# Neighbourhood attention: the softmax reciprocals of twelve of sixteen steps turned and spread by two transfers on Pool's queue in place of a PE transpose

## The chip, the cores and the metric

The kernel runs on one core of a Trainium2 chip. The metric is the device time of one launch in microseconds, the median of several runs; lower is better. The profile is one execution of the same program recorded by the hardware profiler, with its own time. The engines are named as in the profile: PE (matmul), PEld (PE's weight loads), DVE (vector), ACT (scalar), POOL (GpSimd) and SP (whose queue issues most loads).

## The reference, cut to what matters

The reference is a two-layer transformer on 256 latent tokens (a grid of 4 rows by 64 columns) and 256 context tokens, width 1024. Layer 0 mixes with retention, layer 1 with neighbourhood attention; each is followed by a squared-ReLU MLP and layer norms. The change lies in the neighbourhood attention of layer 1, with 32 heads of 32 columns:

```python
s_loc = einsum('bqhd,bikhd->bhqik', q_r, k_band) + bias      # -inf outside the window
s_ctx = einsum('bqhd,blhd->bhql', q_r, k_c)
s = concatenate([s_loc.reshape(...), s_ctx], axis=-1)
prob = softmax(s, axis=-1)
o = einsum('bhqik,bikhd->bqhd', p_loc, v_band) + einsum('bhql,blhd->bqhd', prob[..., band:], v_c)
y_lat = o.reshape(b, n, d) @ w_o
```

The softmax divides by a sum for each query and head. The kernel multiplies the attended values by the reciprocals of these sums at the end.

## The kernel before, in words

The attention is cut into 16 steps (`NS = 16`, line 1438). Step n stands for a group of four heads (g = n // 2) and half of the query columns (qt = n % 2), that is 128 queries on the partitions. What is done for one n:

- `scores(n)` (line 1547): twelve PE matmuls into four PSUM banks, one for each head (tile `pqk` in the profile).
- `soften(n)` (line 1560): DVE adds the bias and takes the minimum for each head, ACT takes the exponential and adds up each row. The result is `Es[n, j]` (tile `s`) and `sums[n]`, 128 queries by 4 heads.
- `invert(n)` (line 1586): DVE takes the reciprocal of `sums[n]` in place and a second DVE instruction copies each of the four columns 32 times into the tile `rr`, 128 by 128.
- `gather(n)` (line 1600): four Pool copies collect 8 columns of each row of the other half of the columns into one block (`pt`, place RAW), and `load_bias(n + 2)` issues four (n even) or eight (n odd) bias transfers on Pool's queue, into `bias` and `G`.
- `flip(n)` (line 1612): PE transposes the exponentials, twelve blocks and then the block that Pool gathered (tile `ppt`); ACT and DVE copy the four banks to `pt`. `flip_sums(n)` (line 1627) adds a fourteenth transpose: it turns `rr` and writes the result into the right part of one half of the PSUM bank `pav`. There each of the 128 rows (head, column of the head) holds the reciprocals of the 128 queries.
- `turned(n)` (line 1633): ACT copies this turned block from PSUM to the SBUF tile `rt`.
- `attend(n)` (line 1638): PE multiplies with the values into the left part of the same half of `pav` (13 matmuls, which the trace shows as 2 and then 24 instructions), DVE multiplies the result by `rt`, and `split` (ACT, then DVE) writes it into `oTh` and `oTl`, as a high and a low part.

The steps are pipelined over each other by the loop at line 1830. Pass n of it holds, in this order: `gather(n+1)`, `turned(n)`, weight loads, `scores(n+2)`, `soften(n+2)`, further PE work from the table `STEPS` (a projection of keys, queries or values, or half of the output projection), `flip(n+1)`, `invert(n+2)`, `attend(n)`. The thirteen passes n = 0 to 12 are written so; step 0 is prepared ahead of the loop, and n = 13 to 15 are closed by the code after it, from line 1848, where `flip_sums`, `turned` and `attend` are called one by one.

What sets the order: in this part of the kernel PE, ACT and DVE keep the order of the program (line 1400 to 1402 switch it on), and so does SP's queue (`PIN`, line 101). Pool does not: the framework orders its instructions, and the trace shows bias transfers between the gather copies. The transfers' waits and all semaphores are set by the framework from the tiles that each instruction reads and writes. The helper class at line 84 issues the instructions, so nearly all carry the line L84, and the tiles tell them apart.

Of the kernel before, what the change touches and what calls it, by code (L numbers as in the profile page):

```python
# [10 lines left out]
F32 = mybir.dt.float32  # L11
# [6 lines left out]
P = 128  # L18
# [9 lines left out]
HD = 32  # L28
# [76 lines left out]
def kernel(  # L105
# [23 lines left out]
    pe, act, dve, pool, sp = (  # L129
        InOrder(tc, getattr(nc, e), e in PIN)  # L130
        for e in ("tensor", "scalar", "vector", "gpsimd", "sync")
    )
# [3 lines left out]
    smp = ec(tc.tile_pool(name="smp", bufs=4))  # L136
# [6 lines left out]
    dram = ec(tc.tile_pool(name="dram", bufs=1, space=DRAM))  # L143
# [8 lines left out]
    def nm(s):  # L152
        uid[0] += 1
        return f"{s}_{uid[0]}"

    def bank(s="ps"):
        return psp.tile([P, 512], F32, tag="ps", name=nm(s))
# [8 lines left out]
    def tsl(t):  # L166
        return slice(t * P, (t + 1) * P)
# [90 lines left out]
    def fetch(n, in_scratch=False, at=None):  # L258

        for src, k, ncol in specs[len(units) : len(units) + max(n, 0)]:  # L260
            raw = rawp.tile([P, k, ncol], F32, tag="raw", name=nm("raw"))
            sp.dma_start(out=raw[:], in_=src.rearrange("(k p) n -> p k n", p=P))
            if len(units) in scaled_units:
                dve.tensor_mul(
                    out=raw[:], in0=raw[:], in1=scale_row[0].unsqueeze(1).broadcast_to([P, k, ncol])
                )
            if in_scratch or len(units) in scratch_units:
                hi, lo = Rows([scr("hi", F32R) for _ in range(k)]), Rows([scr("lo", F32R) for _ in range(k)])
                for i in range(k):
                    act.copy(out=hi[:, i, :], in_=raw[:, i, :])  # L270
                    pending.append((lo[:, i, :], raw[:, i, :], hi[:, i, :]))
                units.append((hi, lo))
                continue
            if at is None:
                hi = hip.tile([P, k, ncol], F32R, tag="hi", name=nm("hi"))
                lo = lop.tile([P, k, ncol], F32R, tag="lo", name=nm("lo"))
            else:
                both = slot(at, [P, 2, k, ncol], F32R, "hilo")
                hi, lo = both[:, 0], both[:, 1]
            act.copy(out=hi[:], in_=raw[:])  # L280
            pending.append((lo[:], raw[:], hi[:]))
            units.append((hi, lo))

    def lows(n=100, eng=None):
        for lo, raw, hi in pending[:n]:
            (eng or dve).tensor_sub(out=lo, in0=raw, in1=hi.bitcast(F32))
        del pending[:n]
# [591 lines left out]
    def part_v(k, a, b):  # L879
# [8 lines left out]
        out=lgn[:, 0], in_=ret_decay[0].rearrange("(o d) h -> o (d h)", o=1).broadcast_to([P, 8])  # L888
# [118 lines left out]
    for h in range(RH):  # L1007
# [102 lines left out]
        for t in range(4):  # L1110
            po = bank("po")
            scs = list(range(4)) if t < 2 else [2, 3]
            for i, sc in enumerate(scs):
# [9 lines left out]
                out=on, in0=po[:], scalar1=mv[:, 0:1], scalar2=r[:], op0=ALU.subtract, op1=ALU.mult  # L1123
# [314 lines left out]
    NS = 16  # L1438
# [106 lines left out]
    sums, rrs, Es, pts, pss = {}, {}, {}, {}, {}  # L1545

    def scores(n):

        g, qt = n // 2, n % 2
        pss[n] = [bank("pqk") for _ in range(4)]  # L1550
        q, k = q_of(g), kTs[g // 2][:, g % 2]
        for i, (a, b) in enumerate(((0, 0), (0, 1), (1, 0))):
            for j in range(4):
                js = slice(32 * j, 32 * j + 32)
                pe.matmul(
                    pss[n][j][:], lhsT=q[js, a, tsl(qt)], rhs=k[js, b, :], start=(i == 0), stop=(i == 2),
                    tile_position=(32 * j, 0),
                )

    def soften(n):  # L1560

        mn = smp.tile([P, 4], F32, tag="mn", name=nm("mn"), bufs=3)
        sm = sums[n] = smp.tile([P, 4], F32, tag="sums", name=nm("sums"), bufs=3)
        for j in range(4):
            s = Es[n, j] = scr("s")
            dve.tensor_tensor_reduce(
                out=s[:].rearrange("p (a t) -> p a t", a=2),
                in0=pss[n][j][:].rearrange("p (a t) -> p a t", a=2),
                in1=bias_ap(n, j),
                scale=1.0,  # L1570
                scalar=3.0e38,
                op0=ALU.add,
                op1=ALU.min,
                accum_out=mn[:, j : j + 1],
            )
            act.activation(
                out=s[:], in_=s[:], func=AF.Exp, scale=-1.0, bias=mn[:, j : j + 1], accum_out=sm[:, j : j + 1]
            )
# [4 lines left out]
    def av_half(n):  # L1583
        return av[0][:, 256 * (n % 2) : 256 * (n % 2) + 256]

    def invert(n):

        rr = rrs[n] = smp.tile([P, 4, HD], F32, tag="rr", name=nm("rr"), bufs=1)
        dve.reciprocal(out=sums[n][:], in_=sums[n][:])
        dve.tensor_copy(out=rr[:], in_=sums[n][:].unsqueeze(2).broadcast_to([P, 4, HD]))  # L1590


# [4 lines left out]
    def pt_at(n, i):  # L1597
        return turns[n % 2][:, tsl(i)]

    def gather(n):  # L1600

        o = 0 if n % 2 else P
        c0 = 24 if n % 2 else 0
        for j in range(4):
            pool.tensor_copy(
                out=pt_at(n, RAW)[:, 32 * j : 32 * j + 32].rearrange("p (r c) -> p r c", r=4),
                in_=Es[n, j][:, o : o + P].rearrange("p (r c) -> p r c", r=4)[:, :, c0 : c0 + 8],
            )
        if n + 2 < NS:
            load_bias(n + 2)  # L1610

    def flip(n, sums_too=True):
        for j in range(4):
            pp = bank("ppt")
            for i, kc in enumerate((n % 2, 2, 3)):
                pe.transpose(pp[:, tsl(i)], Es[n, j][:, tsl(kc)], ident)
            w = 3 * P
            if j == 3:
                pe.transpose(pp[:, tsl(3)], pt_at(n, RAW), ident)
                w = 4 * P  # L1620
            (dve.tensor_copy if j % 2 else act.copy)(
                out=turns[n % 2][:, 3 * j * P : 3 * j * P + w], in_=pp[:, :w]
            )
        if sums_too:
            flip_sums(n)

    def flip_sums(n):
        pe.transpose(av_half(n)[:, P:], rrs[n][:].rearrange("p h d -> p (h d)"), ident)

    oTs = [None]  # L1630
    rts = {}

    def turned(n):

        rts[n] = smp.tile([P, P], F32, tag="rt", name=nm("rt"), bufs=2)
        act.copy(out=rts[n][:], in_=av_half(n)[:, P:])

    def attend(n):

        g, qt = n // 2, n % 2  # L1640
        oTh, oTl = oTs[0]
        po, rt = av_half(n), rts[n]
        pe.matmul(po[:, :P], lhsT=rest_values(n), rhs=pt_at(n, NEAR), start=True, stop=False)
        for i, kc in enumerate((qt, 2, 3)):
            for j in range(4):
                pe.matmul(
                    po[32 * j : 32 * j + 32, :P],
                    lhsT=vtile(kc, g // 4)[:, (4 * (g % 4) + j) * HD : (4 * (g % 4) + j + 1) * HD],
                    rhs=pt_at(n, 3 * j + i),
                    start=False,  # L1650
                    stop=(i == 2),
                    tile_position=(0, 32 * j),
                )
        dve.tensor_mul(out=rt[:], in0=po[:, :P], in1=rt[:])
        hi, lo = (
            o[:, g].rearrange("p (r b c) -> p r b c", r=4, b=2)[:, :, qt] for o in (oTh, oTl)
        )
        split(rt[:].rearrange("p (r c) -> p r c", r=4), hi, lo)
# [121 lines left out]
    soften(1)  # L1780
    v_part(0, 1)
    invert(0)
    flip(0)
    rests = rest_mm(0)
    residual(1, xns[1], gb, dve)
    v_part(0, 2)
    rest_evac(rests)
    invert(1)
    v_part(0, 3)

# [34 lines left out]
    def run(fs):  # L1825
        for f in fs:
            f()

    for n, (early, late, last, before, after) in enumerate(STEPS):
        gather(n + 1)  # L1830
        turned(n)
        fetch(early)
        lows(early)
        scores(n + 2)
        soften(n + 2)
        fetch(late)
        lows(late)
        run(before)
        flip(n + 1)
        invert(n + 2)  # L1840
        fetch(last)
        attend(n)
        run(after)

        lows(100 if n < len(STEPS) - 2 else len(STEPS) - 1 - n)


    n = NS - 1
    gather(n - 1)
    turned(n - 2)  # L1850
    flip(n - 1, False)
    fetch(1)
    attend(n - 2)
# [370 lines left out]
```

## Time and profile before

| what | us |
|---|---|
| median of 3 runs | 1172.66 |
| lowest, highest | 1172.62, 1175.49 |
| profiled execution, its own time | 1173.14 |
| its span, first to last instruction | 1171.0 |
| mean granted PE clock | 0.999 |

The profiled execution lies 2.1 us above its span. The attention with its loop lies between about 815 and 985 us of the span. In the views below, the timeline gives the start in us, the duration in us, then engine, line, operation, and output tile "<-" input tiles with shapes and a count; square brackets hold the idle time ahead and what ended it. A row of a tile gives the shortest, the median and the longest duration in ns and the first and last start. A row of the DMA view gives the output and input, the queue, the count, the size and the median time from issue to landing.

### The profile page before, as it was taken

What the parts mean: (1) busy time and instruction counts of PE and PEld (TensorE: products, weight loads), DVE (VectorE), ACT (ScalarE), POOL (GpSimd) and SP (SyncE); (2) the same over time, 40 slices, a digit from 0 to 9 for tenths busy, and PEclk for the clock granted to TensorE, in tenths of its full rate; (3) what the DMA queues carried; (4) which work ended last, traced back from release to release, by engine and by line L of the source; (5) the groups of instructions that cost most, each with busy time, mean ns of one, the idle gap of its engine ahead of it and who ended that gap; (6) DMA issues with size and microseconds to landing.
All of it is one profiled execution on the core that took longest, in us unless ns stands there. A gap on an engine that the chain in (4) does not pass through costs nothing.

```text
span 1171.0 us, 17545 instructions
## 1 busy us (share of the span) xinstructions
PE 1160.9 (99%) x6687; PEld 980.6 (84%) x6687; DVE 850.3 (73%) x1363; ACT 480.8 (41%) x819; POOL 232.5 (20%) x418
## 2 busy tenths in 40 slices
PE   9999999999999999999999999999999999999997
PEld 7788888888888889888888888889888878999886
DVE  3787687777798877677866675578577589877457
ACT  3643332222323246442122333237466666756341
POOL 0102001010220241781211001223343430000001
PEclk9999999999999999999999999999999999999999
DMA  9943562544365426767666665637344335666761
GB/s 279 277 134 100 162 192 94 158 149 145 108 180 170 140 65 213 195 135 223 190 201 189 205 204 189 202 101 205 82 140 138 108 114 158 214 205 205 239 199 54
DMA packets 140115, 195.10 MB, mean 167 GB/s; under 512 B 9936, under 2 KB 81136, under 8 KB 140032
## 3 DMA queue, kind: packets, MB, share of 16 engines
q1 hardware_dynamic: 131904, 182.03, 50.6%
q0 software_dynamic: 6976, 9.39, 4.0%
q10 hardware_dynamic: 1152, 2.56, 0.7%
q8 instruction: 52, 0.85, 0.3%
q14 instruction: 31, 0.25, 0.1%
HBM read 189.12 MB, written 5.75 MB: 166 GB/s over the span
## 4 chain that ended last, share of the span: by engine, by line
PE 94%; DVE 2%; DMA 1%; ACT 1%; issue 1%; POOL 0%; ACTq 0%; DVEq 0%; SPq 0%
PE p L84 44%; PE pq L84 8%; PE pv L84 8%; PE pw L84 7%; PE pg L84 7%; PE pn L84 5%; PE pnv L84 4%; PE po L84 2%; PE ppt L84 2%; PE pnw L84 1%; PE pS L84 1%; PE pav L84 1%; PE pqk L84 1%; PE pt L84 1%; PE pada L84 1%; PE p1t L84 1%
## 5 line engine op out<-in xcount | busy, mean ns | idle before, releaser
L84 ACT CAST hi<-raw 128x1024 fp32r<-128x1024 f32 (+2 forms) x228 | 231.7, 1032 | 306.1 <-PE p L84 111.0
L84 DVE TENSOR_TENSOR lo<-raw,hi 128x1024 fp32r<-128x1024 f32 (+2 forms) x228 | 272.2, 1210 | 87.5 <-ACT hi L84 87.2
L84 PE MATMUL p<-hi,hid 128*128 128x512 f32 (+1 forms) x780 | 238.0, 386 | 0.0
L84 PEld LDWEIGHTS p<-hi,hid 128*128 128x128 f32 x780 | 145.8, 188 | 29.5
L84 PE MATMUL p<-hTl,hi 128*128 128x256 f32 (+1 forms) x512 | 165.9, 326 | 0.0
L84 PE MATMUL p<-hTh,lo 128*128 128x256 f32 (+1 forms) x512 | 165.9, 326 | 0.0
L84 PE MATMUL p<-hTh,hi 128*128 128x256 f32 (+1 forms) x512 | 162.6, 327 | 0.0
L84 PE MATMUL p<-lo,hid 128*128 128x512 f32 (+1 forms) x390 | 150.5, 386 | 0.0
L84 DVE SCALAR_TENSOR_TENSOR acc<-rawa,scol,acc 128x1024 f32<-128x1024 f32 x56 | 73.6, 1321 | 65.2 <-DMA rawa<-in_ada_w_dram 65.0
L84 PEld LDWEIGHTS p<-hTl,hi 128*128 128x128 f32 x512 | 96.5, 188 | 8.7
L84 PEld LDWEIGHTS p<-hTh,lo 128*128 128x128 f32 x512 | 96.4, 188 | 8.7
L84 PEld LDWEIGHTS p<-hTh,hi 128*128 128x128 f32 x512 | 94.2, 188 | 8.8
L84 PEld LDWEIGHTS p<-lo,hid 128*128 128x128 f32 x390 | 73.3, 188 | 14.5
L84 DVE SCALAR_TENSOR_TENSOR strips<-rawa,scol,strips 128x512 f32<-128x512 f32 x112 | 78.6, 763 | 0.0
L84 ACT CAST hid<-r 128x256 fp32r<-128x256 f32 (+1 forms) x64 | 31.9, 500 | 108.5 <-DVE r L84 108.5
L84 POOL TENSOR_TENSOR rstd<-rstd,misc 128x1 f32<-128x1 f32 x28 | 19.1, 684 | 219.6 <-DVE rstd L84 218.6
L84 ACT ACTIVATE s<-s,mn 128x512 f32<-128x512 f32 x64 | 45.5, 713 | 21.6 <-DVE mn L84 21.6
L84 PE MATMUL pw<-hi,oh 128*128 128x512 f32 x128 | 50.8, 397 | 0.0
L84 PE MATMUL pg<-hi,hTh 128*128 128x512 f32 x128 | 50.6, 395 | 0.0
L84 PE MATMUL pw<-hi,ol 128*128 128x512 f32 x128 | 50.1, 391 | 0.4 <-DVE ol L84 0.4
L84 PE MATMUL pg<-hi,hTl 128*128 128x512 f32 x128 | 49.9, 390 | 0.0
L84 PE MATMUL pw<-lo,oh 128*128 128x512 f32 x128 | 49.8, 389 | 0.0
(243 smaller groups left out, 2275.4 us busy)
## 6 DMA issues: line engine op xcount, KB each, us to landing
raw<-in_mlp_w_dram SPq DMA_DIRECT2D x128, 512.0 KB, 4.5
rawa<-in_ada_w_dram SPq DMA_DIRECT2D x80, 512.0 KB, 3.9
raw<-in_ret_w_in_dram SPq DMA_DIRECT2D x42, 512.0 KB, 4.1
raw<-in_nat_w_in_dram SPq DMA_DIRECT2D x24, 512.0 KB, 4.3
rawq<-in_ada_w_dram SPq DMA_DIRECT2D x16, 512.0 KB, 5.9
raw<-in_ret_w_o_dram SPq DMA_DIRECT2D x16, 512.0 KB, 3.7
bias<-rpb_rows POOLq DMA_DIRECT2D x32, 128.0 KB, 2.9
raw<-in_nat_w_o_dram SPq DMA_DIRECT2D x8, 512.0 KB, 4.0
```

What stands on the lines that cost most here:

```text
L84: r = f(*args, **kwargs)
```

## The change

A DRAM tile `rsums` of 16 × 4 × 128 numbers is added. For n in 1 to 12 (`BY_DMA`) the second DVE instruction of `invert`, the transpose of `flip_sums` and the ACT copy of `turned` are left out. In their place `send_sums(n)`, called in pass n − 1 behind `gather(n)`, issues two transfers on Pool's queue. The first writes the 128 by 4 reciprocals to DRAM as 4 rows of 128, so each number is a run of its own. The second reads these four rows back into `rt`, each one 32 times, so that 128 partitions get a row of 128 numbers. The second reads what the first wrote. `attend(n)` multiplies by `rt` as before. Steps 0, 13, 14 and 15 stay as they were.

```diff
+    rsums = dram.tile([NS, 4, P], F32, tag="rsums", name="rsums")
+    BY_DMA = range(1, 13)
+
+    def send_sums(n):
+        if n not in BY_DMA:
+            return
+        row = rsums[n]
+        rts[n] = smp.tile([P, P], F32, tag="rt", name=nm("rt"), bufs=2)
+        pool.dma_start(out=row.rearrange("j q -> q j"), in_=sums[n][:])
+        pool.dma_start(out=rts[n][:], in_=bass.AP(row.tensor, row.offset, [[P, 4], [0, HD], [1, P]]))
+
     def invert(n):
 
+        dve.reciprocal(out=sums[n][:], in_=sums[n][:])
+        if n in BY_DMA:
+            return
         rr = rrs[n] = smp.tile([P, 4, HD], F32, tag="rr", name=nm("rr"), bufs=1)
-        dve.reciprocal(out=sums[n][:], in_=sums[n][:])
         dve.tensor_copy(out=rr[:], in_=sums[n][:].unsqueeze(2).broadcast_to([P, 4, HD]))
...
-        if sums_too:
+        if sums_too and n not in BY_DMA:
             flip_sums(n)
...
     for n, (early, late, last, before, after) in enumerate(STEPS):
         gather(n + 1)
-        turned(n)
+        if n not in BY_DMA:
+            turned(n)
+        send_sums(n + 1)
```

## Prediction

> **What bounds the kernel now.** I read the page first, for the engine shares and the chain that ended last.
>
> ```profile
> span 1171.0 us, 17545 instructions
> PE 1160.9 (99%) x6687; PEld 980.6 (84%) x6687; DVE 850.3 (73%) x1363; ACT 480.8 (41%) x819; POOL 232.5 (20%) x418
> PE 94%; DVE 2%; DMA 1%; ACT 1%; issue 1%; POOL 0%; ACTq 0%; DVEq 0%; SPq 0%
> ```
>
> TensorE is busy for 99% of the span and carries 94% of the chain. The edit touches only the thirteen loop steps of the attention, so I took the busy times of the stretch in which the twelve changed steps lie, then its chain in order of time.
>
> ```profile
> core 0: us, PE busy (x) PEld busy (x) DVE busy (x) ACT busy (x) POOL busy (x), PEclk, DMA share, GB/s
> 840.00:956.00 116.00, 116.00 (x1004) 95.25 (x997) 79.96 (x203) 74.95 (x182) 49.95 (x121) 1.00 0.45 127
> ...
> 849.75 5.68 PE pn L84 x24
> 855.43 1.42 PE ppt L84 x13
> 856.85 1.12 PE pav L84 x27
> 857.97 0.90 PE pqk L84 x10
> ...
> 958.12 2.93 ACT s L84 x8
> 961.05 0.37 ACT pt L84
> 961.47 0.98 PE ppt L84 x7
> ```
>
> PE is busy for all 116 us, at granted clock 1.00, and a step is one unbroken PE queue: projection (pn), flip (ppt), attend (pav), scores (pqk). Only at 961, behind the last exponentials, does the chain pass ACT and come back to PE. So the price of a step is what PE must issue, as long as nothing PE needs comes late. The Trainium skill, "Perfetto Trace Analysis", section "Identifying the Most-Contended Engine", warns that matmul busy time misleads because matmuls are pipelined, and counts weight-load time instead. By that count PE has room here (95.25 of 116 us), and taking PE work out could give nothing. The starts of the instructions decide between the two, so I read those.
>
> **What leaves.** Twelve steps lose a DVE spread, a PE transpose and an ACT copy:
>
> ```profile
> L84 DVE COPY rr<-sums x16: 226/227/298, 823.9 to 969.8; 128x128 f32<-128x128 f32 x16
> L84 PE MATMUL pav<-cst,rr x16: 272/273/329, 827.7 to 970.0; 128*128 128x128 f32 x16
> L84 ACT COPY rt<-pav x16: 258/262/272, 840.2 to 970.5; 128x128 f32<-128x128 f32 x16
> ...
> 864.38 1.47 PE L84 MATMUL ppt<-cst,s 128*128 128x128 f32 x12
> 865.69 0.27 PE L84 MATMUL ppt<-cst,pt 128*128 128x128 f32 x1
> 865.80 0.27 PE L84 MATMUL pav<-cst,rr 128*128 128x128 f32 x1
> 865.90 0.39 PE L84 MATMUL pav<-pt,G 128*128 128x128 f32 x2
> ...
> 874.80 0.27 PE L84 MATMUL ppt<-cst,pt 128*128 128x128 f32 x1
> 874.91 0.27 PE L84 MATMUL pav<-cst,rr 128*128 128x128 f32 x1
> 875.02 0.39 PE L84 MATMUL pav<-pt,pt 128*128 128x128 f32 x2
> ```
>
> The transpose lasts 273 ns, but the next matmul starts 0.10 us (865.80 to 865.90) or 0.11 us (874.91 to 875.02) after it, because they overlap. The twelve transposes ahead have the same pitch: (865.69 − 864.38) / 12 = 0.109. There is no gap on either side that another wait could be hiding in. So PE wins 12 × 0.105 = 1.26 us. The duration would give 12 × 0.273 = 3.3 us; that is the far bound of the gain on PE, and 0 the near one; I take the pitch, since it is read at the place itself.
>
> DVE wins 12 × 0.227 = 2.7 us and ACT 12 × 0.262 = 3.1 us. In the stretch DVE works 79.96 and ACT 74.95 of 116 us beside a full PE, so this is hidden and I count nothing. The exception is the return to PE at 961:
>
> ```profile
> 938.65 0.23 DVE L84 COPY rr<-sums 128x128 f32<-128x128 f32 x1
> ...
> 957.84 1.47 PE L84 MATMUL ppt<-cst,s 128*128 128x128 f32 x12
> 959.15 0.27 PE L84 MATMUL ppt<-cst,pt 128*128 128x128 f32 x1
> ...
> 960.48 1.86 PE L84 MATMUL ppt<-cst,s 128*128 128x128 f32 x12
> 962.18 0.27 PE L84 MATMUL ppt<-cst,pt 128*128 128x128 f32 x1
> ```
>
> One flip takes 1.31 us (957.84 to 959.15), the next 1.70 (960.48 to 962.18): PE waits 0.39 us for step 14's exponentials and the ACT copy that frees a bank. The late steps are short on PE, so the DVE and ACT queues run nearly full from about 938 on. Nine of the twelve transposes lie ahead of that (0.95 us, passed on whole, as the chain there is still PE) and three beside it (0.32 us, which this wait may take back). Of DVE's and ACT's twelve pieces only the spread of n = 11, at 938.65, lies on that chain, and its 0.23 us come off it too. So PE arrives 1.26 us earlier, what it waits for about 1.18: the wait grows by up to 0.1, at most 0.32. I take 0.1. **Sum: −1.26 + 0.1 ≈ −1.2 us**, with ends −3.3 and, if all that is won is given back at this wait, 0.
>
> **What comes.** Each of twelve steps gets two transfers on Pool's queue: 2 KB to DRAM as 512 runs of one 4-byte number, then 64 KB back in rows of 512 bytes. The second reads what the first wrote, so Pool must wait for the landing between them. Behind that wait on Pool's queue stand the next step's four gather copies and its bias transfers (4 or 8). Pool's rows:
>
> ```profile
> 855.38 2.13 POOL L84 DMA_DIRECT2D G<-rpb_rows  x4
> 861.56 0.21 POOL L84 COPY pt<-s 128x32 f32<-128x32 f32 x1 [4.05 <-ACT s L84]
> ...
> 863.37 0.53 POOL L84 COPY pt<-s 128x32 f32<-128x32 f32 x2
> 863.91 1.73 POOL L84 DMA_DIRECT2D bias<-rpb_rows  x3
> 871.52 0.21 POOL L84 COPY pt<-s 128x32 f32<-128x32 f32 x1 [5.87 <-ACT s L84]
> ...
> 858.56 0.17 DVE L84 RECIPROCAL sums<-sums 128x4 f32<-128x4 f32 x1
> ...
> 877.76 0.28 DVE L84 TENSOR_TENSOR rt<-pav,rt 128x128 f32<-128x128 f32 x1
> ```
>
> The reciprocal at 858.56 is that of n = 3; Pool then idles until 861.56, so the first transfer can be issued at about 858.8. Its price must be bounded from the nearest transfers:
>
> ```profile
> rpb_rows<-rpb_neg POOLq DMA_DIRECT2D x49, 14.0 KB, 3.7
> rpb_rows<-rpb_neg POOLq DMA_DIRECT2D x2, 0.9 KB, 3.6
> G<-rpb_rows POOLq DMA_DIRECT2D x32, 32.0 KB, 3.0
> ...
> L84 POOL DMA_DIRECT2D rpb_rows<-rpb_neg x79: 594/594/789, 474.9 to 523.7; - x79
> ...
> DMA to landing us min/median/max: 2.0/3.1/6.8
> ```
>
> The 0.9 KB row is 32 heads × 7 rows of one number (line 411): 224 runs of 4 bytes, from DRAM to DRAM, landed 3.6 us after issue; 224 runs of 64 bytes took 3.7. The size of a run is thus nothing here; the number of runs may be something. The low end for the new transfer is 2.0 (the fastest of this tile's transfers); if all above 2.0 went by the number of runs it would be 2.0 + 1.6 × 512/224 = 5.7; the slowest transfer that touches this tile took 6.8. I take 3.6, the row with the same kind of run. Then Pool is held for 3.6 + 0.59 (issue of the second, by the 594 ns row) = 4.2 us a step. It has 116 − 49.95 = 66 us idle in the stretch, 5.5 for each of the twelve sends. It fits, and a late step eats only cover: the gather copies of n = 4 end at 863.90 and their flip turns them at 874.80, 10.9 us later. The new operand has still more: sent at 858.8, on its way back at 862.4, landed 3.0 later (the 32 KB row) at 866, and DVE multiplies by it at 877.76. **Charge: 0.** If that cover were gone, each further us that Pool is late is a us of PE, since the flip stands ahead of all else on PE's queue. The 12 × 66 KB that come through DRAM, 0.8 MB, stand beside 116 us × 127 GB/s = 15 MB; the weight loads they share the DMA engines with end in none of PE's waits above. I charge nothing.
>
> The rule that speaks against the edit is in the Trainium skill, "DMA: Bandwidth & Descriptors", section "Rules for kernel authors": a last dimension that isn't contiguous costs one descriptor per element, and turning by a rearranged plain transfer is given as 19 times worse than the transpose made for it. The 4-byte row beside the 64-byte row bears out a cost that doesn't sink with the bytes, and no run so far shows 512 of them. By the rule, this would come out as the slower rival below.
>
> **The rivals.**
> *Pool falls behind (slower).* A first transfer slow per run holds Pool beyond its idle time, and lateness adds up over twelve steps until the gather copies miss their flip. It decides where 12 × (L + 0.59 − 5.5) exceeds 10.9, that is from L = 5.8 us. At the slowest row, L = 6.8: 12 × 1.89 − 10.9 = 11.8 us late, less 1.2, so +10.6: 1183.3 us. For it: 5.7 by runs is close to that point. Against it: the 4-byte row is at 3.6, and the order on Pool isn't written out, so gather copies may be put between the two transfers. Chance 0.10.
> *Absorbed (no change).* The wait at 961, or another engine's queue behind a full PE, takes the gain back: 1172.7 us. For it: the 0.39 us wait already there. Against: only three transposes lie beside it. This is also what weight-load time as the measure of PE would give. Chance 0.13.
> *DVE and ACT count (faster).* If each step ended with the DVE and ACT queues, the gain would be 12 × (0.227 + 0.262) = 5.9 us: 1166.8. Against: PE without a gap in 116 us. Chance 0.05.
>
> **How the numbers follow.** The profiled execution took 1173.14 us, 2.1 around its span of 1171.0; it lies 0.5 above the median of 1172.66 (lowest 1172.62, highest 1175.49). On the profiled time the forecast is 1171.9, on the median 1171.5. Chance of the forecast case: 0.72. The range goes from 1169.4 (1172.66 − 3.3, the far bound of PE's gain) to 1173.8 (absorbed, and 1.1 more for the median of runs that lie 2.9 apart); with these two cases it holds 0.85, less a little for the spread of the runs. A measurement can tell about 0.3%, 3.5 us, from no change. Faster by that needs the DVE and ACT case: 0.05. Slower needs Pool's: 0.10. The forecast and the absorbed case both lie within: 0.85.
>
> **What would show it.** Right: PE x6675, the pitch from the flip's last transpose to the first pav matmul 0.11 instead of 0.21, 16 − 12 = 4 rr copies and 4 rt copies, the attention stretch shorter by about 1.2 us, all other stretches unchanged. On Pool, a wait of about 3 us for the rsums transfer twelve times, with gather copies still ending long before their flip. Wrong: the first transfer landing later than 5.8 us after issue, PE weight loads of the flip waiting for Pool's pt copy, DVE waiting for a transfer ahead of the rt multiply, or a flip at 961 that waits much longer than 0.39 us.

## The result, and the profile after

| what | before | after |
|---|---|---|
| median of 5 runs, us | 1172.66 | 1238.00 |
| lowest, highest, us | 1172.01, 1175.49 | 1235.71, 1238.59 |
| profiled execution: own time, span, us | 1173.14, 1171.0 | 1238.00, 1236.2 |
| mean granted PE clock | 0.999 | 0.974 |

The kernel is 1.0548 times as slow, interval 1.0533 to 1.0563, or 65 us. The forecast of 1171.5 us had the direction wrong, and the time lies far outside its range. The page of after:

```profile
PE 1177.4 (95%) x6675; PEld 990.1 (80%) x6675; DVE 849.1 (69%) x1351; ACT 479.5 (39%) x807; POOL 251.0 (20%) x442
...
PEclk9999999999999999999999999999886978999999
```

The twelve transposes are gone (x6675 for x6687), and yet PE is busy 16.5 us longer; the row of the clock has a hole where the attention is. PE's idle time went from 1171.0 − 1160.9 = 10.1 us to 1236.2 − 1177.4 = 58.8. So the span's 65.2 us are 48.7 us in which PE waits and 16.5 us in which it works more slowly. The windows place both. First before, then after, in the columns of the prediction's window row:

```profile
838.00:973.00 135.00, 134.88 (x1197) 110.19 (x1196) 95.39 (x242) 87.12 (x212) 52.69 (x130) 1.00 0.43 126
```

```profile
838.00:1040.00 202.00, 152.49 (x1193) 120.45 (x1192) 96.15 (x233) 87.22 (x204) 71.29 (x154) 0.85 0.41 90
940.00:960.00 20.00, 5.71 (x60) 3.77 (x61) 3.18 (x13) 1.33 (x5) 10.51 (x26) 0.57 0.28 60
960.00:980.00 20.00, 20.00 (x150) 17.18 (x149) 11.89 (x27) 12.37 (x27) 6.19 (x10) 1.00 0.46 104
```

Nearly the same PE work (twelve transposes fewer, and eight other matmuls more at the ends of the stretch) takes 202 us instead of 135, 152.49 of them busy at a granted clock of 0.85. The second row is the worst place: PE has 5.71 us of work in 20, and the clock is at 0.57. In the 20 us behind it PE has no wait, and the clock is at 1.00 again. From 470 to 838 us PE is busy throughout in both kernels, at clock 1.00.

What PE waits for, in the waits of after between 820 and 1060 us (total, times, longest):

```profile
POOL rt L84 <- issue: 53.9, 6, 10.7
...
PE ppt L84 <- POOL pt L84: 36.5, 8, 8.5
...
POOL rt L84 <- DMA rsums<-sums: 18.7, 2, 9.5
...
PE pnv L84 <- POOL sel L84: 12.9, 1, 12.9
...
DVE rt L84 <- DMA rt<-rsums: 10.4, 5, 3.9
```

Two waits of PE for Pool come to 36.5 + 12.9 = 49.4 us, about the whole of the new idle time; before, PE waited for Pool nowhere in this stretch. Pool waits ahead of its second transfer (output `rt`). The waiting is for the landing of the first transfer even where the view puts it down to "issue" or to another engine, as the DMA view for the same stretch and Pool's timeline show:

```profile
raw<-in_nat_w_o_dram SPq DMA_DIRECT2D x8, 512.0 KB, 10.4
...
rsums<-sums POOLq DMA_DIRECT2D x12, 2.0 KB, 9.7
```

```profile
930.44 0.79 POOL L84 DMA_DIRECT2D rsums<-sums  x1
939.32 0.73 POOL L84 DMA_DIRECT2D rt<-rsums  x1 [8.10 <-issue]
940.05 0.36 POOL L84 COPY pt<-s 128x32 f32<-128x32 f32 x2
...
951.89 0.73 POOL L84 DMA_DIRECT2D rt<-rsums  x1 [8.16 <-issue]
...
955.46 0.36 POOL L84 COPY sel<-cst 128x32 f32<-128x32 f32 x2
```

The 2 KB write lands 9.7 us after issue. Pool stands for it (930.44 to 939.32), then issues the read back, and only then copies the next gather block. From the issue of the first transfer to that of the second the twelve steps hold Pool 10.1 us in the mean (121.2 / 12, between 8.9 and 12.1). PE's timeline shows the price in the same place:

```profile
936.61 1.47 PE L84 MATMUL ppt<-cst,s 128*128 128x128 f32 x12
941.34 0.33 PE L84 MATMUL ppt<-cst,pt 128*128 128x128 f32 x1 [3.26 <-POOL pt L84]
...
955.74 1.08 PE L84 MATMUL pnv<-R,sel 128*32 128x128 f32 x16 [12.95 <-POOL sel L84]
```

The flip is ready but for the block that Pool gathers, and waits 3.26 us for it. The 12.95 us are for a tile of which the prediction doesn't speak, `sel`: `rest_mm` (line 1667), called once from `STEPS` in the middle of the loop, has two Pool copies into it, and these stood behind the next pair of transfers. In the before kernel they had next to no cover:

```profile
911.79 0.36 POOL L84 COPY sel<-cst 128x32 f32<-128x32 f32 x2 [0.88 <-PE ppt L84]
```

They ended at 912.15, and PE used them at 913.69. The sixteen matmuls that use them lasted 272 ns each there, and 418 ns each in after, right behind the 12.95 us of waiting.

The DMA view holds a second effect: SP's loads `raw<-in_nat_w_o`, which the edit doesn't touch, take 10.4 us now. The DMA view of before, between 815 and 990 us:

```profile
raw<-in_nat_w_o_dram SPq DMA_DIRECT2D x8, 512.0 KB, 4.0
bias<-rpb_rows POOLq DMA_DIRECT2D x28, 128.0 KB, 2.9
```

### The profile page after: what moved, and what is told of

It reads as the page before. It is cut to its first block, busy times and chain, and to the rows that moved or that the text cites. A ratio compares the mean times of both kernels' runs of the same rounds, so it can differ in the third digit from the quotient of the medians.

```text
span 1236.2 us, 17570 instructions
## 1 busy us (share of the span) xinstructions
PE 1177.4 (95%) x6675; PEld 990.1 (80%) x6675; DVE 849.1 (69%) x1351; ACT 479.5 (39%) x807; POOL 251.0 (20%) x442
## 6 DMA issues: line engine op xcount, KB each, us to landing
raw<-in_nat_w_o_dram SPq DMA_DIRECT2D x8, 512.0 KB, 10.4
```

## The experiments

The theory after the result: the first transfer is slow to land, Pool is held by it, and what stands behind on Pool's queue reaches PE late. Rivals: the other transfers are late because of these writes, and PE waits for that; the wait would cost nothing in another order; the spread form of the operand (each row read 32 times), or the 64 KB read, costs by itself. Where a kernel ran only once, its time is read to some 3 us.

**No transfers: `e5_no_transfers`.** It asks for the gain alone.

```diff
-        pool.dma_start(out=row.rearrange("j q -> q j"), in_=sums[n][:])
-        pool.dma_start(out=rts[n][:], in_=bass.AP(...))
+        pool.memset(rts[n][:], 1.0)
```

> The changed kernel without both transfers: twelve steps have neither spread, transpose, ACT copy nor transfers, and rt is filled with ones by a Pool memset, so the values stay undivided. This is the worth of what is taken out, by itself. By the pitch of PE's starts (12 x 0.105 us, 0.1 taken back): 1.2 us less than before, ratio 0.999. If the work taken out is hidden: 1.000. If the duration of the transposes or DVE's and ACT's share counted: 0.995 to 0.997.

Measured: 1170.69 us, ratio 0.9988 (0.9980 to 0.9997). By the ratio that is −1.4 us, against the prediction's −1.2. PE's starts agree. In the chain that ended last two scores of successive steps start at

```profile
857.07 0.90 PE pqk L84 x8
...
866.08 0.91 PE pqk L84 x11
```

that is 9.01 us apart. In before the same two lie 9.12 apart, at 857.97 (shown in the prediction) and

```profile
867.09 0.90 PE pqk L84 x9
```

A step is shorter by 0.11 us, the pitch of a transpose, and not by the 0.27 us for which one lasts. All that is lost comes with the transfers.

**The same 2 KB in 128 runs of 16 bytes: `e1_rows16`.** The first transfer keeps its bytes, its wait and its place; only what it writes beside what changes, so the read back gets the numbers in another order.

```diff
-        pool.dma_start(out=row.rearrange("j q -> q j"), in_=sums[n][:])
+        pool.dma_start(out=bass.AP(row.tensor, row.offset, [[4, P], [1, 4]]), in_=sums[n][:])
```

> The changed kernel, but the first transfer writes the 128 by 4 reciprocals as they lie, 128 runs of 16 bytes in one block of 2 KB, instead of 512 runs of 4 bytes. The second transfer is the same and so reads the numbers in the wrong order; the output is not the reference's. Theory A (the 4-byte runs make the first transfer slow, and Pool's wait for it holds the gather copies): the first transfer lands in 2.5 to 4 us instead of the median 9.7, Pool's time fits its idle time again, and the kernel comes to 1170 to 1174 us. Theory B (any first transfer that Pool must wait for costs about 10 us here, whatever its runs, since it queues behind the bias transfers): landing still 8 to 10 us and 1225 to 1240 us.

Measured: 1172.95 us, ratio 0.9989 (0.9977 to 1.0000). The DMA view:

```profile
rsums<-sums POOLq DMA_DIRECT2D x12, 2.0 KB, 2.7
```

With a landing of 2.7 us the whole loss is gone, with both transfers, Pool's wait and the 64 KB read still there. So the edit's other parts cost nothing that the times show (PE waits 1.7 us for `sel`), and the way the first transfer writes costs 65 us.

**The second transfer one pass later: `e3_later`.**

```diff
+    def bring_back(n): ...   # the second transfer of send_sums
...
         gather(n + 1)
...
+        bring_back(n)
         send_sums(n + 1)
```

> The changed kernel, but the second transfer of step n is issued one pass later, behind the gather copies of that pass, so that Pool needn't wait for the first transfer with the copies queued behind. Both transfers are the same in size and runs. If Pool's wait is the loss, the waits of PE for Pool's copies vanish and the kernel comes to 1171 to 1180 us although the first transfer still lands in about 10 us. If the transfer's own presence is the loss (it slows the weight loads and the bias transfers, whose landing times went from 4.0 to 10.4 and from 2.9 to 4.0 us), the time stays above 1200 us.

Measured: 1235.93 us, ratio 1.0518 (1.0497 to 1.0538). This tells nothing of the question. Pool's order is the framework's, and it set the transfer back to where it had been, as Pool's timeline shows:

```profile
838.04 0.82 POOL L84 DMA_DIRECT2D rsums<-sums  x1 [8.47 <-DVE sums L84]
847.53 0.74 POOL L84 DMA_DIRECT2D rt<-rsums  x1 [8.66 <-DMA rsums<-sums]
848.26 0.36 POOL L84 COPY pt<-s 128x32 f32<-128x32 f32 x2
```

**The first transfer alone: `e4_first_only`.** The kernel before, with the twelve writes and nobody who reads them, so Pool has no read back that must wait for them.

```diff
+        if n in range(1, 13):
+            row = rsums[n]
+            pool.dma_start(out=row.rearrange("j q -> q j"), in_=sums[n][:])
```

> The kernel before with only the twelve first transfers added (512 runs of 4 bytes each on Pool's queue); nothing reads what they write and no work is taken out. With Pool's wait as the loss: 1172 to 1176 us, landing about 10 us. With the transfer's presence as the loss: weight loads land in about 10 us instead of 4 and the time rises by 20 us or more.

Measured: 1180.68 us, ratio 1.0057 (1.0037 to 1.0076), that is 6.7 us. The DMA view between 815 and 1050 us:

```profile
raw<-in_nat_w_o_dram SPq DMA_DIRECT2D x8, 512.0 KB, 10.8
bias<-rpb_rows POOLq DMA_DIRECT2D x28, 128.0 KB, 8.4
...
rsums<-sums POOLq DMA_DIRECT2D x12, 2.0 KB, 9.5
```

Without a read back the write still takes 9.5 us, and other transfers land late with it: the bias, 2.9 us in before, takes 8.4, and the loads 10.8. The time lies between the two that were expected: the writes alone cost a tenth of the loss. Even this tenth is not shown to come from the late loads. In the waits the longest of PE is again for Pool, which stands for landings here too, ahead of bias transfers into `G`; for weights PE waits 0.3 us.

```profile
POOL G L84 <- DMA rsums<-sums: 14.6, 3, 6.6
...
PE pnv L84 <- POOL sel L84: 2.8, 1, 2.8
```

**Pool held without a slow transfer: `e13_hold`.** The fast write of `e1_rows16`, then 35 memsets on Pool before the read back, with Pool kept in the order of the program.

```diff
+        pool.dma_start(out=bass.AP(row.tensor, row.offset, [[4, P], [1, 4]]), in_=sums[n][:])
+        hold = smp.tile([P, 4, HD], F32, tag="rr", name=nm("hold"), bufs=1)
+        for _ in range(35):
+            pool.memset(hold[:], 0.0)
```

> The changed kernel with the fast first transfer (128 runs of 16 bytes, landing 2.7 us; wrong order of numbers) and 35 memsets of a scratch tile on Pool, about 7 us, between the two transfers, with Pool in the order of the program in the loop. Pool is held as long as in the change, but no slow transfer is in flight. If Pool's hold makes most of the loss: 12 x (7 + 0.7 + 0.6 + about 1 of wait - 5.5) - 11 = 35 us and more, 1205 to 1235 us, with the granted clock falling as in the change. If the slow writes' effect on the other transfers makes it: below 1190 us.

Measured: 1230.53 us, ratio 1.0490 (1.0475 to 1.0504). Pool's timeline, PE's waits and the DMA view:

```profile
851.07 0.59 POOL L84 DMA_DIRECT2D rsums<-sums  x1
851.66 9.18 POOL L84 MEMSET hold<- 128x128 f32 x35
861.16 0.72 POOL L84 DMA_DIRECT2D rt<-rsums  x1 [0.33 <-issue]
```

```profile
PE ppt L84 <- POOL pt L84: 26.3, 6, 6.6
...
PE pnv L84 <- POOL sel L84: 10.9, 1, 10.9
DVE rr L84 <- POOL hold L84: 10.7, 1, 10.7
...
PE ppt L84 <- DVE mn L84: 6.5, 1, 6.5
```

```profile
raw<-in_nat_w_o_dram SPq DMA_DIRECT2D x8, 512.0 KB, 4.6
```

The memsets hold Pool 10.1 us a step (851.07 to 861.16), as long as the slow write does. The loads land about as before (4.6 us, for 4.0), and still 57.5 us are lost, most of them at the same two waits of PE. The third wait, 6.5 us for `mn`, is the experiment's own: `hold` takes the one buffer of `rr`, so that DVE's copy into `rr` for step 13 stood 10.7 us for the memsets, and `mn` behind it. Without it some 51 us are left, about four fifths of the loss. So the hold is the main loss. How the rest divides isn't shown: the writes alone cost 6.7 us, and Pool's order is another one here.

**Why the write is slow.** The row that the prediction took as nearest also wrote runs of 4 bytes, 224 of them, and landed in 3.6 us. Three things differ: that row reads from DRAM and not from SBUF, the number of runs, and that its targets lie 128 bytes apart (a column of rows of 32 numbers), where the new write fills rows of 128 numbers side by side. Five kernels, each run once and all writing from SBUF, tell these apart. `e7_runs128` and `e8_runs256` send only one or two of the four heads. `e9_spread`, `e11_stride16` and `e12_stride8` send all 512 numbers, but to places 64, 16 and 8 bytes apart; the region is filled with ones ahead of the steps, and these are read back. (`e2_spread`, which is `e9_spread` without the ones, gave no result.)

```diff
# e7_runs128 (e8_runs256 with 0:2)
+        pool.dma_start(out=row[0:1].rearrange("j q -> q j"), in_=sums[n][:, 0:1])
# e9_spread (e11_stride16 with 4 and e12_stride8 with 2 in place of 16)
+    rsums = dram.tile([NS, 4, P, 16], F32, tag="rsums", name="rsums")
+        pool.dma_start(out=row[:, :, 0].rearrange("j q -> q j"), in_=sums[n][:])
```

> The changed kernel, but the first transfer sends only the first head's 128 numbers, 128 runs of 4 bytes, and the second reads this one row 128 times; three of four heads get the wrong reciprocals. If the landing time is a fixed part and a part for each 4-byte run (512 runs land in 9.7 us, a 2 KB transfer of 128 longer runs in 2.7), it is 2.7 + 7.0 x 128/512 = 4.4 us here and Pool's time fits: 1171 to 1175 us. If the second transfer's wait or another fixed cost made up the 9.7 us, landing stays above 8 us.

> As the kernel with 128 runs, but two heads' 256 numbers are sent and each row is read 64 times. By a cost for each run: landing 2.7 + 7.0 x 256/512 = 6.2 us, which with 0.73 and 0.79 us of issue is above Pool's 5.5 us of idle time a step, so lateness adds up by about 1.5 us a step, 18 us over twelve, of which 11 are covered: 1175 to 1185 us. By a threshold between 256 and 512 runs: landing below 5 us and 1171 to 1174 us.

> The changed kernel, but every one of the 512 numbers of the first transfer goes to a place of its own in DRAM, 64 bytes from the next, instead of one beside the other. The region is filled with ones once, by two transfers of 256 KB on ACT's queue ahead of the steps, and the second transfer reads the first 2 KB of a step's part, so its numbers are not the reciprocals. If it is the number of 4-byte runs that costs, landing stays near 9.7 us and the time near 1236 us. If it is that many 4-byte writes fall into the same few lines of DRAM and wait for each other, landing falls to 3 to 5 us and the time to 1170 to 1180 us.

> As the kernel with the 512 numbers 64 bytes apart in DRAM (landing 2.8 us), but 16 bytes apart, so that four of them share 64 bytes instead of sixteen as in the change; the second transfer reads the first 2 KB of the step's part, which was filled with ones, so the output isn't the reference's. If each write into the same 64 bytes waits for the one before it, landing is 2.8 + (9.7 - 2.8) x 3/15 = 4.2 us and the time 1172 to 1176 us. If sharing alone makes the loss, however few share: 8 to 10 us and 1215 to 1240 us.

> As the kernel with the 512 numbers 16 bytes apart in DRAM, which landed in 2.9 us, but 8 bytes apart, so that two of them share 16 bytes and eight share 64; the second transfer reads ones. If the writes collide when they share 64 bytes, and four in a line were too few to show: 4 to 7 us. If they collide only when they share a smaller piece, such as 8 bytes: 2.5 to 3.2 us and 1172 to 1177 us. If sharing 16 bytes is enough for the whole loss: 8 to 10 us.

The DMA views, in this order:

```profile
rsums<-sums POOLq DMA_DIRECT2D x12, 0.5 KB, 8.3
```

```profile
rsums<-sums POOLq DMA_DIRECT2D x12, 1.0 KB, 8.3
```

```profile
rsums<-sums POOLq DMA_DIRECT2D x12, 2.0 KB, 2.8
```

```profile
rsums<-sums POOLq DMA_DIRECT2D x12, 2.0 KB, 2.9
```

```profile
rsums<-sums POOLq DMA_DIRECT2D x12, 2.0 KB, 4.0
```

The times were 1219.54, 1219.88, 1175.02, 1176.65 and 1181.01 us. A quarter of the runs lands in 8.3 us, hardly sooner than all 512 (9.7). All 512, 16 bytes apart or more, land in 2.8 to 2.9; 8 bytes apart in 4.0. So it is not the count, nor SBUF as the source, but how close the 4-byte targets lie. Their size counts too: side by side, 128 runs of 4 bytes take 8.3 us (`e7_runs128`) and 128 runs of 16 bytes 2.7 (`e1_rows16`). At 4.0 us the kernel already loses 8 us in its one execution, nearly all of it at the `sel` copies (PE waits 8.1 us there).

Where in the transfer does the time go? The DMA view between the first issue and just before its landing, first of after (from 838.2 to 848.4 us), then of `e9_spread` (837.6 to 840.3), in 40 slices each:

```profile
DMA  0000006000000000000000010000006055332033
...
q0 software_dynamic: 32, 0.00, 1.8%
...
rsums<-sums POOLq DMA_DIRECT2D x1, 2.0 KB, 10.0
```

```profile
DMA  0000000000000000000005964000000000000000
...
q0 software_dynamic: 32, 0.00, 6.9%
...
rsums<-sums POOLq DMA_DIRECT2D x1, 2.0 KB, 2.3
```

Both show 32 packets, moved in one burst about 1.4 us after issue (slice 7 of 0.255 us: 839.7; slice 22 of 0.068 us: 839.0). Then this queue moves nothing more; the engines' work from slice 24 on is that of another queue, a load of SP issued at 843.00. One landing comes soon after the burst, the other 8 us later. The time is not spent in moving bytes. What the chip does in it, the trace doesn't show.

**The wait moved with Pool's order kept: `e10_later_pinned`.** `e3_later` with Pool held to the order of the program in the loop (`pool.on = True`), so that the next gather copies and bias transfers stand ahead of the read back.

> The changed kernel with the second transfer of step n issued one pass later, and now with Pool kept in the order of the program in the loop, so that each pass has four gather copies, the bias transfers, the second transfer of the step whose first one was sent a pass before, and the next first transfer. In the earlier run without the pinned order the framework had moved the second transfer up again, right behind the first, so that run did not part the two causes. If Pool's wait with the gather copies behind it is the main loss: the waits of PE for Pool's pt copies fall below 10 us in total and the time is 1174 to 1185 us, the rest being the slow transfer's presence (the kernel before with only the first transfers lost 6 us). If its presence is the main loss: above 1200 us.

Measured: 1202.02 us, ratio 1.0244 (1.0215 to 1.0273). The waits:

```profile
POOL rt L84 <- DMA rsums<-sums: 29.8, 5, 7.4
...
DVE rt L84 <- DMA rt<-rsums: 25.9, 7, 10.6
...
PE pn L84 <- ACT hi L84: 7.3, 1, 7.3
```

The order wins back more than half of the loss, and PE no longer waits for `pt` or `sel`. But the time lies above 1200, as was expected if the presence of the slow writes is the main loss; it is `e13_hold` that speaks for the hold. Pool and DVE wait for landings still, since in this kernel the write takes 10.1 us and the bias 9.4. PE's longest wait, 7.3 us for a cast of weights, goes back to such a landing: ACT stood for DVE's multiply by `rt`, and DVE stood 10.6 us for the read back. So the slow write costs by a second way, the late operand, once the first is closed. How the 29 us that are left divide, this run doesn't tell.

**A version that lands fast and is right in order.** `e6_dve_turn` lets DVE write the reciprocals eight times side by side and turn blocks of 32 by 32, so that the first transfer writes 128 runs of 128 bytes. `e14_turn_later` adds the later read back with Pool's order kept; `e15_turn_sel` instead puts the `sel` copies on DVE.

```diff
+            dve.reciprocal(out=rr[:, 0].rearrange("p (r j) -> p r j", j=4),
+                           in_=sums[n][:].unsqueeze(1).broadcast_to([P, 8, 4]))
+            dve.transpose(out=rr[:, 1], in_=rr[:, 0])
...
+        pool.dma_start(out=row.rearrange("i (b c) -> b i c", b=4), in_=rrs[n][:, 1])
```

> The changed kernel with the reciprocals turned on DVE ahead of the first transfer: the reciprocal writes its four columns eight times (128 by 32), DVE transposes the four blocks of 32 by 32, and the first transfer writes 128 runs of 128 bytes instead of 512 of 4. The second transfer is that of the change. If many small writes into the same lines of DRAM are the cause, the first transfer lands in 2.5 to 4 us, Pool never holds the gather copies up, and the kernel gets what the change was worth without it: 1.2 us less than before, ratio 0.998 to 1.000. If a first transfer of 16 KB from 128 partitions is slow as well: above 1180 us.

> The kernel with the turn on DVE (128 runs of 128 bytes, landing 2.6 us), with two edits: the second transfer is issued one pass later and Pool keeps the order of the program in the loop, so Pool waits for no landing; and DVE takes the reciprocal of four columns and copies them eight times (in place of a reciprocal of 32 columns, 343 ns). In the run without these, one wait on Pool was left on PE, 1.9 us for the sel copies of the second rest_mm. If that wait was all that stood against the 1.2 us: 1170.5 to 1172 us, ratio 0.998 to 1.000, and PE waits for no Pool instruction. If Pool's pinned order brings a new wait (the sel copies now stand behind the transfers of their pass): 1173 to 1178 us.

> The kernel with the turn on DVE, the order of Pool left to the framework and the second transfer right behind the first, but the four sel copies made by DVE instead of Pool, and the reciprocal of four columns copied eight times. If the wait for sel was what the turn on DVE lost: 1170.5 to 1172.5 us, ratio 0.998 to 1.000. If DVE's longer chain (reciprocal, copy and transpose) makes the loss: 1173 to 1176 us with PE waits on DVE's pt copies or on ACT.

Measured: 1175.53 us, ratio 1.0025 (1.0015 to 1.0036); 1173.91, 1.0009 (1.0000 to 1.0018); 1175.49, 1.0027 (1.0017 to 1.0038). The write of `e6_dve_turn` takes

```profile
rsums<-rr POOLq DMA_DIRECT2D x12, 16.0 KB, 2.6
```

for eight times the bytes. The loss is gone but for 1 to 3 us, and none of the three beats the kernel before. Small waits can take the 1.4 us back: PE waits 1.9 us for `sel` in the first, 2.2 in two waits in the third, and 1.4 us for `rt` at ACT's copy (`turned`) in the second. What makes up the rest of the 4 us between `e6_dve_turn` and the kernel without transfers stays open: `e15_turn_sel` was to win it by freeing `sel`, and did not.

## Why the prediction was wrong, point by point

**The failed step is the price of the first transfer, L.** The prediction took 3.6 us "the row with the same kind of run", with 6.8 as the far bound; it measured 9.7, outside both. "The size of a run is thus nothing here; the number of runs may be something" is wrong on both counts for runs side by side: 128 runs land in 8.3 us with 4 bytes each and in 2.7 with 16, while four times as many runs of 4 bytes take only 9.7, and 2.8 when they stand apart. The chosen row was alike in the size of its runs and unlike in what decides, the distance between them, and that could have been read in the code: line 411 and the write below it fill one column in rows of 32 numbers. The slowest row of the trace is no upper bound for a form of access that the trace doesn't hold.

The rule quoted from the Trainium skill, "DMA: Bandwidth & Descriptors", section "Rules for kernel authors", spoke on the right side. But its reason, one descriptor per element, does not part the cases: 512 separate elements landed in 2.8 us 64 bytes apart and in 9.7 side by side.

**The rival "Pool falls behind" is what happened**, beyond the price that it was given. With L = 9.7, and with the 0.73 us that the issue of the second transfer took, its own working gives 12 × (9.7 + 0.73 − 5.5) − 10.9 = 48.3 us, and PE's new idle time is 48.7. The agreement is partly luck: 12.9 us of the 48.7 stand at the `sel` copies, which it doesn't hold. With 8.3 us it gives 31.5, where `e7_runs128` had 36.0 us more idle time on PE (1217.4 − 1171.3 − 10.1). The threshold of 5.8 us was too high too, as at 4.0 us the `sel` copies were already late (`e12_stride8`). Three of the signs of being wrong that the prediction named came: a landing later than 5.8 us, the flip waiting for Pool's `pt` copy, and DVE waiting for a transfer ahead of the multiply by `rt` (10.4 us, which PE doesn't feel in after).

**"Charge: 0" named too little cover.** The 10.9 us ahead of the flip were real: with a landing of 4.0 us PE waits for no `pt` (`e12_stride8`). But Pool's queue holds two rarer entries, the `sel` copies, with 1.5 us of cover. PE waits 1.5 us for them at a landing of 2.9 us (`e11_stride16`) and 8.1 at 4.0, so even the 3.6 us of the prediction would hardly have been free. And "gather copies may be put between the two transfers" did not come true, but for one copy in the last step: the read back stands ahead of the next gather copies, in `e3_later` even against the program's order.

**The clock was left out.** The granted clock was 0.85 in the stretch, and 16.5 us of the 65.2 are PE working more slowly: a quarter of the loss, for which no rival had a term. The low clock goes with PE's waits and not with the slow writes: `e13_hold`, with a fast write and 43.8 us of PE idle between 838 and 1030 us, has 0.87 there, and `e4_first_only`, with the slow write and 3.4 us idle between 838 and 983, has 0.99.

**The 0.8 MB beside 15 MB, charged with nothing,** looked at bytes. The writes made other transfers land up to 7 us later, and alone, with nobody who reads them, they cost 6.7 us (`e4_first_only`).

**Right** were the bound (PE's queue without a gap), the gain by pitch and not by duration (`e5_no_transfers`: −1.4 for the predicted −1.2, not −3.3), that DVE's and ACT's shares count for nothing, and the 64 KB read: with the fast write of `e1_rows16` DVE waits for it nowhere ahead of the multiply by `rt`.

## What to carry to other kernels

Price a transfer by where its runs land, not by its bytes or their number alone: a turned write that puts 4-byte numbers of many partitions side by side is a form of its own, and a row for spread runs says nothing of it. Where an engine's queue must stand for a landing, list everything that is queued on it, the entries that come once included, with the cover of each, and take the smallest as the point from which it costs. A waiting PE paid twice here, 48.7 us by the waits and 16.5 by the lower clock that went with them.

## What the runs showed of the hardware that was not expected

512 numbers of 4 bytes land 9.7 us after issue when they lie side by side in DRAM, 4.0 when 8 bytes apart, and 2.9 and 2.8 when 16 and 64 bytes apart; 128 runs of 16 bytes, side by side, land in 2.7. The packets are moved about 1.4 us after issue in the slow and in a fast case alike, and in the slow one the landing comes 8 us later. The Trainium skill, "DMA: Bandwidth & Descriptors", says in its table of specifications that the DMA engine does a read-modify-write for less than 512 bytes; these runs neither show that nor exclude it, since spread runs of 4 bytes are as far below 512 and land fast. While such writes are under way, other transfers land late as well: the eight 512 KB loads `raw<-in_nat_w_o` took 10.8 us instead of 4.0 in `e4_first_only`, with the same traffic but for 12 × 2 KB.
